# Two encoder layers on one Trainium2 core: norm factors applied behind the first product, projections scaled at eviction, residual rows in large loads, and new spans for the attention

## The chip, the core and the metric

The kernel runs on one core of a Trainium2 chip. The core has TensorE (PE, matrix products into PSUM), VectorE (DVE), ScalarE (ACT), GpSimd (POOL), and SyncE (SP), whose queue issues nearly all DMA transfers here. Each engine works through its own list of instructions in the order in which it stands. The metric is the time of one execution in microseconds (us); lower is better.

## What is computed

Two layers of a streaming encoder over 1024 prompt tokens and 32 sample tokens, model width 1024. Before and behind every sublayer stands an RMS norm; the residual is added behind the second one.

```python
def rms_norm(x, g):
    xf = x.astype(jnp.float32)
    y = xf * lax.rsqrt(jnp.mean(xf * xf, axis=-1, keepdims=True) + EPS)
    return (y * g.astype(jnp.float32)).astype(x.dtype)

def layer_prompt(x, mem, p, t5_table, lam_init):
...
    z = split_in(rms_norm(x, g[N_MIX_PRE]), p['w_in'])
...
    x = x + rms_norm(jnp.concatenate([a, b, c], axis=-1) @ p['w_out'], g[N_MIX_POST])
    mk, mv = mem_kv(mem, g[N_MEM], p['w_mk'], p['w_mv'])
    x, conv_state = tail_sublayers(x, mk, mv, jnp.zeros((B, CONV_W - 1, D_FF), x.dtype), p)

def tail_sublayers(x, mk, mv, conv_past, p):
    g = p['norms']
    x = x + rms_norm(cross_attention(rms_norm(x, g[N_X_PRE]), mk, mv, p['w_xq'], p['w_xo']), g[N_X_POST])
    f, conv_state = conv_ffn(rms_norm(x, g[N_F_PRE]), conv_past, p['w_gate'], p['w_up'],
                             p['conv_w'], p['conv_b'], p['w_down'])
    return x + rms_norm(f, g[N_F_POST]), conv_state
```

`a`, `b` and `c` are three groups of attention heads (differential, banded, latent), which read parts of `z`. The sample tokens attend to caches of 1024 older tokens.

## The kernel before

**Tiles.** Activations lie with the model width on the partitions: eight tiles of 128 rows, one column for each token. The tokens are cut into two halves, h = 0 of 544 columns (the chunks g = 0 and 1, of 256 and 288; the 32 sample tokens sit in the second) and h = 1 of 512 (two chunks of 256). A product runs in fp32r: every operand is split into a high part (`hi`, a copy, line 118 on ACT) and a low part (`lo`, the difference, line 137 on POOL or 135 on DVE), and `mm3` (lines 217 to 219) issues three matmuls for each pair of tiles. `unit` is one 128-row tile of a product over the whole width: 24 matmuls into one PSUM tile `ps_g`.

**Names of stages.** The text calls project(l,h) the input projection of a layer and half (22 tiles of w_in), attention (l,h) what `attend` does, cross (l,h) what `cross` does: the output projection w_out with its norms, the query product w_xq, the cross attention into 256 memory tokens, its product w_xo with its norms; ffn (l,h) is the gated MLP, and its end `finish` is the last down product with its norms.

**Two streams.** `run` makes one program out of two generators. `dense` yields project(0,0), the first norm of half 1, the memory keys, project(0,1), and then ffn(l,h) and project(l+1,h) in turn. `latent` yields for each (l,h) the attention and then the cross. `par` always continues the generator whose time, summed from the yields, is behind: a positive yield is PE work, a negative one is waiting, and a yielded function holds the generator until it is true. `paced` spreads the attention over `SPANS`; `slowed(gen, k)` adds waiting of k times the work; `ffn` starts when `"done" in F[l, h]`. So these numbers alone decide how many matmuls of the dense stream stand in PE's list beside one step of the latent stream. What stands there is called filler here.

**Norms.** `sum_squares` squares eight tiles on ACT (line 244) and adds them on DVE and POOL (line 246); `inv_rms` sums over the partitions by a matmul with `ones` (line 254, on PE) and takes the inverse root on ACT (lines 233 and 234). `prenorm` waits for this factor r, multiplies x, gain and r (line 399, DVE) and splits; all of it stands ahead of the first product. `prenorm_late` (cross and ffn) splits x times gain at once and issues the sum of squares and the matmul of line 254 behind that but ahead of the first product; the product is multiplied by r at its eviction. `postnorm` multiplies by gain and r (line 469) and adds the residual (line 470), which `residual` loads by four DMAs of two tiles (`xr`, two buffers) for each chunk.

**Evictions.** The projections' PSUM tiles are copied by ACT (`z_k`, `z_v`, `z_cq`, `z_ckv`) or split by ACT and DVE (`z_q`). The gate product of the ffn is multiplied by r in line 1652 on DVE.

## Time and profile before

| | us |
|---|---|
| median of three runs | 3716.85 (3716.11 to 3724.8) |
| the profiled execution, its own time | 3728.03 |
| its span in the trace | 3725.5 |
| PE busy | 3266.1 (88%) |
| DVE, ACT, POOL busy | 2073.0, 1836.3, 2080.5 |

The span runs from the first to the last recorded instruction; the profiled execution took 11.18 us more than the median. PE is the busiest engine. A matmul is pipelined with its neighbours, so a busy PE is not always a PE at its peak; the count of matmuls in a stretch tells more than the busy time.

### The profile page before, as it was taken

The page shows a single profiled execution, that of the slowest core. Times are in us where ns is not written, and L with a number is a line of the kernel's source. Part 1 is how long each engine was busy: PE and PEld are TensorE (multiplying, and loading weights), DVE is VectorE, ACT ScalarE, POOL GpSimd, SP SyncE. Part 2 cuts the span into 40 slices and gives each one's busy share as a digit, 9 for nine tenths or more (in the row PEclk, how much of TensorE's full clock was granted, in tenths as well). Part 3 has the DMA queues.
Part 4 walks back from the last instruction along what each step waited for, and adds up shares of the span by engine and source line. Part 5 has one row for each costly group of instructions (what it writes and reads, how often), then busy time and mean ns, then how long its engine had stood idle before and what let it go on. Part 6 is the DMA issues. An engine that isn't in the chain of part 4 may idle for free.

```text
span 3725.5 us, 66150 instructions
## 1 busy us (share of the span) xinstructions
PE 3266.1 (88%) x24536; PEld 3099.4 (83%) x24536; DVE 2073.0 (56%) x4627; ACT 1836.3 (49%) x3926; POOL 2080.5 (56%) x1868
## 2 busy tenths in 40 slices
PE   6997997699999799759999969959999998579997
PEld 5986896599999699659999959959998998579996
DVE  4665316576676743365666562557787654554444
ACT  3565535555454545455445453466555453543332
POOL 5444545476665545546665565656565466556654
PEclk9997997799999799879999989979999999789998
DMA  7665643133333455413334444433344343122222
GB/s 221 215 187 152 205 158 121 63 109 93 110 110 104 143 183 173 132 56 108 118 121 127 134 132 164 165 112 105 105 125 119 109 122 120 53 80 86 86 86 80
DMA packets 246505, 464.79 MB, mean 125 GB/s; under 512 B 42513, under 2 KB 136105, under 8 KB 246185
## 3 DMA queue, kind: packets, MB, share of 16 engines
q1 hardware_dynamic: 243736, 457.07, 39.1%
q8 instruction: 194, 3.18, 0.3%
q0 software_dynamic: 2448, 3.51, 0.3%
q14 instruction: 127, 1.03, 0.1%
HBM read 365.93 MB, written 97.66 MB: 124 GB/s over the span
## 4 chain that ended last, share of the span: by engine, by line
PE 64%; DVE 14%; ACT 7%; DMA 6%; issue 4%; POOL 4%; SPq 1%; POOLq 0%; ACTq 0%; DVEq 0%
PE ps_g L217 17%; PE ps_g L218 17%; PE ps_g L219 16%; DVE gt L1676 4%; PE ps_g L575 3%; DVE pg L469 2%; PE ps_g L651 2%; PE ps_g L650 1%; PE ps_g L254 1%; PE ps_sc L716 1%; DMA xr<-x 1%; ACT wh L118 1%; DVE pg L412 1%; POOL wl L137 1%; DVE zn L246 1%
## 5 line engine op out<-in xcount | busy, mean ns | idle before, releaser
L217 PE MATMUL ps_g<-pg,wh 128*128 128x256 f32 (+1 forms) x4352 | 1260.2, 290 | 20.2 <-ACT pg L118 17.1
L218 PE MATMUL ps_g<-pg,wh 128*128 128x256 f32 (+1 forms) x4352 | 1251.9, 288 | 5.3 <-POOL pg L137 3.9
L219 PE MATMUL ps_g<-pg,wl 128*128 128x256 f32 (+1 forms) x4352 | 1246.2, 286 | 0.0
L137 POOL TENSOR_TENSOR wl<-wr,wh 128x1024 fp32r<-128x1024 f32 (+1 forms) x368 | 885.6, 2411 | 457.7 <-ACT wh L118 437.2
L217 PEld LDWEIGHTS ps_g<-pg,wh 128*128 128x128 f32 x4352 | 828.4, 190 | 30.2 <-ACT pg L118 20.2
L218 PEld LDWEIGHTS ps_g<-pg,wh 128*128 128x128 f32 x4352 | 826.6, 190 | 10.0 <-POOL pg L137 5.3
L219 PEld LDWEIGHTS ps_g<-pg,wl 128*128 128x128 f32 x4352 | 822.9, 189 | 0.2
L118 ACT ACTIVATE wh<-wr 128x1024 fp32r<-128x1024 f32 (+1 forms) x368 | 383.4, 1053 | 555.7 <-PE ps_g L218 402.9
L217 PE MATMUL ps_g<-hs,wh 128*128 128x256 f32 (+1 forms) x1424 | 417.4, 299 | 45.3 <-DVE pg L1712 39.7
L218 PE MATMUL ps_g<-hs,wh 128*128 128x256 f32 (+1 forms) x1424 | 410.7, 290 | 4.5 <-POOL hs L137 4.4
L219 PE MATMUL ps_g<-hs,wl 128*128 128x256 f32 (+1 forms) x1424 | 408.2, 289 | 0.0
L673 ACT ACTIVATE pg<-ps_sc,sm 128x640 f32<-128x640 f32 (+7 forms) x384 | 278.0, 729 | 125.0 <-DVE sm L724 73.8
L217 PEld LDWEIGHTS ps_g<-hs,wh 128*128 128x128 f32 x1424 | 271.2, 193 | 64.6 <-DVE pg L1712 48.7
L1676 DVE SCALAR_TENSOR_TENSOR gt<-gt,cst,gt 128x32 f32<-128x32 f32 (+3 forms) x264 | 272.3, 1050 | 74.5 <-ACT gt L1671 73.2
L1712 DVE TENSOR_TENSOR pg<-pg,ps_g 128x256 f32<-128x256 f32 (+1 forms) x640 | 260.3, 422 | 89.4 <-PE ps_g L219 87.2
L118 ACT ACTIVATE pg<-ps_g 128x512 fp32r<-128x512 f32 (+3 forms) x480 | 209.2, 455 | 186.4 <-PE ps_g L575 171.9
L135 DVE TENSOR_TENSOR pg<-ps_g,pg 128x512 fp32r<-128x512 f32 (+2 forms) x448 | 225.7, 518 | 101.7 <-ACT pg L118 99.3
L218 PEld LDWEIGHTS ps_g<-hs,wh 128*128 128x128 f32 x1424 | 275.7, 194 | 7.1 <-POOL hs L137 6.1
L219 PEld LDWEIGHTS ps_g<-hs,wl 128*128 128x128 f32 x1424 | 275.5, 193 | 0.2
L217 PE MATMUL ps_g<-pg,pg 128*128 128x256 f32 (+1 forms) x768 | 229.0, 299 | 5.2 <-ACT pg L118 5.2
L575 PE MATMUL ps_g<-ident,pg 128*128 128x128 f32 x1232 | 200.9, 291 | 34.0 <-POOL pg L1550 26.6
L219 PE MATMUL ps_g<-pg,pg 128*128 128x256 f32 (+1 forms) x768 | 225.2, 295 | 1.1 <-POOL pg L137 1.0
(243 smaller groups left out, 6281.5 us busy)
## 6 DMA issues: line engine op xcount, KB each, us to landing
wr<-i_w_in SPq DMA_DIRECT2D x88, 512.0 KB
wr<-i_w_gate SPq DMA_DIRECT2D x88, 512.0 KB
wr<-i_w_up SPq DMA_DIRECT2D x88, 512.0 KB
wr<-i_w_down SPq DMA_DIRECT2D x88, 512.0 KB
pg<-i_w_out SPq DMA_DIRECT2D x32, 512.0 KB
qt<-aq SPq DMA_DIRECT2D x192, 64.0 KB
pg<-av SPq DMA_DIRECT2D x24, 512.0 KB
pg<-ak SPq DMA_DIRECT2D x96, 128.0 KB
```

The lines of the kernel that those rows point to most:

```text
L118: nc.scalar.activation(out, in_, AF.Copy)
L135: nc.vector.tensor_sub(out, in_, h)
L137: nc.gpsimd.tensor_sub(out, in_, h)
L217: nc.tensor.matmul(out, wh, xh, start=(i == 0), stop=False)
L218: nc.tensor.matmul(out, wh, xl, start=False, stop=False)
L219: nc.tensor.matmul(out, wl, xh, start=False, stop=(i == n - 1))
L469: nc.vector.scalar_tensor_tensor(ys[k], ys[k], self.gain(l, which, k), r, op0=ALU.mult, op1=ALU.mult)
L575: self.nc.tensor.transpose(q[:, i * 128 : i * 128 + 128], e[:, c : c + 128], self.ident)
L651: nc.tensor.matmul(p[:, a:b], v(kt), aT[1][s // 4][:, s % 4, a:b], start=False, stop=(i == n - 1))
L673: self.nc.scalar.activation(e[:, :n], sc, AF.Exp, bias=m, scale=-1.0, accum_out=z)
L1676: nc.vector.scalar_tensor_tensor(cv[:, a:b], gp[:, a + o - e : b + o - e], conv_col(f, tap), cv[:, a:b], op0=ALU.mult, op1=ALU.add)
L1712: nc.vector.tensor_add(y[m][:, cols(g)], y[m][:, cols(g)], p)
```

## The change

The second norm form, `prenorm`, goes; `prenorm_late` is used everywhere, and no longer issues the matmul of line 254 itself: it leaves it in `late[chunk]`, and `now` issues it right behind the first unit of the product that follows. The projections' evictions therefore multiply by the factor r (`Xr`), on DVE; the high parts of queries and keys move to ACT and the low part of queries to POOL. `residual` is replaced by `chunk_load`: two or three DMAs for a chunk, issued ahead of the norm, into `pg` pages or, at the end of the ffn, into `gt`, `u` and `hs` tiles. `outputs` loads the attention's results in the same way. The four spans shrink, a page is added (`NPG`) and an `xr` buffer taken, the w_xq loads are issued later, the ffn may start as soon as both its inputs are named, and the cross is slowed by 0.5 in its inner part in place of 1.0 in all. The number of matmuls stays the same.

```diff
-SPANS = (220.0, 480.0, 400.0, 380.0)
+SPANS = (180.0, 400.0, 340.0, 350.0)
...
-NPG = 26
+NPG = 27
...
-    def prenorm(self, xs, l, which, w, out, pages, lo=("pool",)):
-
-        nc = self.nc
-        acc = self.sum_squares(xs, w)
-        yield -5
-        r = self.inv_rms(acc, self.ones, 1024.0, w)
-        yield -2
-        xh, xl = pages()
-        for k in range(KT):
-            a = self.t("st")[:, :w]
-            nc.vector.scalar_tensor_tensor(a, xs[k], self.gain(l, which, k), r, op0=ALU.mult, op1=ALU.mult)
-            self.hi("act", xh[k], a)
-            self.lo(lo[k % len(lo)], xl[k], a, xh[k])
-        out.extend((xh, xl))
-        yield -4
-
-    def prenorm_late(self, xs, l, which, w, r, out, pages):
+    def prenorm_late(self, xs, l, which, w, r, out, pages, late, chunk, wait=0):
+
 
         nc = self.nc
         xh, xl = pages()
@@ -414,8 +399,17 @@
                 yield -2
         acc = self.sum_squares(xs, w)
         out.extend((xh, xl))
-        yield -4
-        self.inv_rms(acc, self.ones, 1024.0, w, r=r)
+        late[chunk] = lambda: self.inv_rms(acc, self.ones, 1024.0, w, r=r)
+        yield -2
+        if wait:
+            yield -wait
+            self.now(late, chunk)
+
+    @staticmethod
+    def now(late, g):
+        f = late.pop(g, None)
+        if f:
+            f()
...
+    def chunk_load(self, src, g, tiles=None):
+
+        w, out = width(g), []
+        if tiles is None:
+            n = 2 * HW[0] // w
+            tiles = [(self.t("pg"), min(n, KT - k)) for k in range(0, KT, n)]
+        for page, n in tiles:
+            x = page[:, : n * w].rearrange("p (k c) -> p k c", k=n)
+            k = len(out)
+            self.dma(x, src[k : k + n, :, span(g)].rearrange("k p c -> p k c"))
+            out += [x[:, i] for i in range(n)]
         return out
 
-    def postnorm(self, ys, l, which, src, g, out, store=None):
+    def postnorm(self, ys, l, which, xs, g, out, store=None):
...
-        xs = self.residual(src, g) if not isinstance(src, list) else src
+        yield -7
...
             g = 2 * h + c
             p = self.ps("g")[:m, : width(g)]
             self.unit(w, self.Xc[c], p, m)
+            self.now(self.late, g)
             evac(p, g)
...
+        nc, r = self.nc, self.Xr
         def evac(p, g):
-            self.hi("act", z[:, 0, cols(g)], p, scale)
-            self.lo("dve", z[:, 1, cols(g)], p, z[:, 0, cols(g)], scale)
+            cs = cols(g)
+            a = self.t("st")[:, : width(g)]
+            nc.vector.scalar_tensor_tensor(a, p, scale, r[:, cs], op0=ALU.mult, op1=ALU.mult)
+            self.hi("act", z[:, 0, cs], a)
+            self.lo("pool", z[:, 1, cs], a, z[:, 0, cs])
...
-            nc.scalar.activation(raw[:, cs], p, AF.Copy)
-            self.hi("dve", z[:, 0, cs], raw[:, cs])
+            nc.vector.tensor_mul(raw[:, cs], p, r[:, cs])
+            self.hi("act", z[:, 0, cs], raw[:, cs])
...
-                nc.scalar.activation(raw[:, cols(g)], p, AF.Copy)
+            def evac(p, g, raw=raw):
+                nc.vector.tensor_mul(raw[:, cols(g)], p, r[:, cols(g)])
...
+            nc.gpsimd.tensor_mul(a, a, rx[:32, cs])
...
         def split(p, a):
             self.hi("act", oh[p], a)
             self.lo("pool", ol[p], a, oh[p])
 
-        xs = load(0) + load(2)
-        yield -2
+        xs = list(enumerate(self.chunk_load(d.od, g)))
+        yield -3
...
-        for p, a in load(4) + load(6):
+        for p, a in xs[4:]:
...
-            if m + 1 < KT:
-                ws = split(raw)
+                yield -1.5
+                if m + 1 < KT and g == G[0]:
+                    nxt = split(raw)
+            ws = nxt
         O.clear()
         del pages
-        raws = [load("w_xq", m) for m in range(2)]
...
+            xs = self.chunk_load(d.xin, g)
+            yield from self.postnorm(ys, l, 1, xs, g, ys)
+            del xs
             if g == G[0]:
-                yield -3
-                wq.extend(split(raw) for raw in raws)
-            yield from self.postnorm(ys, l, 1, d.xin, g, ys)
+                raws = [load("w_xq", m) for m in range(2)]
             if g == G[1]:
                 yield lambda: ("q", G[0]) in done
             xn = []
-            yield from self.prenorm_late(ys, l, 2, w, rr[:, cs], xn, lambda: self.chunk_pages(w))
-            yield -2
+            late = {}
+            yield from self.prenorm_late(ys, l, 2, w, rr[:, cs], xn, lambda: self.chunk_pages(w), late, g)
             if not q:
+                wq.extend(split(raw) for raw in raws)
                 q.extend(self.pair_pages())
+                yield -3
             for m in range(2):
                 p = self.ps("g")[:, :w]
                 self.unit(wq[m], xn, p)
+                self.now(late, g)
                 a = self.t("st")[:, :w]
                 nc.vector.scalar_tensor_tensor(a, p, scale, rr[:, cs], op0=ALU.mult, op1=ALU.mult)
                 self.hi("act", q[0][m][:, cs], a)
@@ -1595,7 +1597,7 @@
...
             F[g] = []
-            yield from self.prenorm_late(ys, l, 4, w, F["r"][:, cols(g)], F[g], lambda: fp(g))
+            yield from self.prenorm_late(ys, l, 4, w, F["r"][:, cols(g)], F[g], lambda: fp(g), F["late"], g, 10)
 
         fp = self.half_pages()
         wx = []
-        yield from self.par(*[self.seq(queries(g), attention(g % 2), rest(g)) for g in G])
-        F["done"] = True
+        yield from self.slowed(self.par(*[self.seq(queries(g), attention(g % 2), rest(g)) for g in G]), 0.5)
...
             self.unit(wts["g", f], F[g], p)
+            self.now(F["late"], g)
...
+        last = l + 1 == DEPTH
+        if not last:
+            self.Xc, self.late, self.Xr = [[], []], {}, self.t("r")
         pages = self.half_pages()
 
         def finish(g):
             ys = [t[:, cols(g)] for t in y]
+            if g == gs[0]:
+                xs = self.chunk_load(d.x2, g, [(self.t("gt"), 2) for _ in range(3)] + [(self.t("u"), 2)])
             yield from down_units(k, ws, g)
-            yield from self.postnorm(ys, l, 5, d.x2, g, ys, d.x3)
-            if l + 1 < DEPTH:
-                yield from self.prenorm(ys, l + 1, 0, width(g), self.Xc[g % 2], lambda: pages(g), ("pool", "dve"))
+            if g == gs[1]:
+                xs = self.chunk_load(d.x2, g, [(self.t("hs"), n) for n in (3, 3, 2)])
+            yield from self.postnorm(ys, l, 5, xs, g, ys, d.x3)
+            if not last:
+                yield from self.prenorm_late(ys, l + 1, 0, width(g), self.Xr[:, cols(g)], self.Xc[g % 2], lambda: pages(g),
+                                             self.late, g)
 
...
-                yield lambda: "done" in F[l, h]
+                yield lambda: all(F[l, h].get(g) for g in (2 * h, 2 * h + 1))
...
-                yield from self.slowed(self.cross(l, h, F[l, h]), 1.0)
+                yield from self.cross(l, h, F[l, h])
```

In the rows below an operation is shown as its line in that version, then output<-inputs by the program's names, then the shape.

**PE, cross (0,1), between the last w_out product (ps_g_17822) and the first query product.** In the version before, in its last rows `ps_g_18009` is that query product:

```order
L217 MATMUL ps_g_17822<-pg_16547,pg_17792 128x256
L218 MATMUL ps_g_17822<-pg_16551,pg_17792 128x256
L219 MATMUL ps_g_17822<-pg_16547,pg_17793 128x256
L254 MATMUL ps_g_17911<-zn_17853,ones 128x256
L254 MATMUL ps_g_17940<-zn_17882,ones 128x256 x2
L254 MATMUL ps_g_18002<-zn_17981,ones 128x256
L217 MATMUL ps_g_18009<-pg_17961,pg_17874 128x256
L218 MATMUL ps_g_18009<-pg_17963,pg_17874 128x256
L219 MATMUL ps_g_18009<-pg_17961,pg_17875 128x256
```

In the changed version, the same engine where the sums of squares (zn, ones) of the first postnorm and of the chunk behind it stand; `ps_g_17341` and `ps_g_17377` are units of project(1,0):

```order
L217 MATMUL ps_g_17341<-pg_15190,wh_17270 128x256
L218 MATMUL ps_g_17341<-pg_15194,wh_17270 128x256
L219 MATMUL ps_g_17341<-pg_15190,wl_17271 128x256
L254 MATMUL ps_g_17367<-zn_17221,ones 128x256 x2
L254 MATMUL ps_g_17372<-zn_17246,ones 128x256
L217 MATMUL ps_g_17377<-pg_15187,wh_17270 128x288
L218 MATMUL ps_g_17377<-pg_15191,wh_17270 128x288
L219 MATMUL ps_g_17377<-pg_15187,wl_17271 128x288
```

Before, three sums of squares stand one behind the other between the w_out product and the query product. Now units of the projection stand on both sides of them; in all, the matmuls of other stages between the last w_out and the first w_xo product of a cross go from 221 to 494 in cross (0,0), from 0 to 400 in (0,1), from 666 to 1062 in (1,0) and from 0 to 52 in (1,1).

**PE, the start of ffn (0,0), behind cross (0,0).** Before (L716 are scores of the attention (0,1), `ps_g_7997` is the first gate unit):

```order
L254 MATMUL ps_g_7800<-zn_7712,ones 128x256 x2
L254 MATMUL ps_g_7866<-zn_7805,ones 128x288 x2
L716 MATMUL ps_sc_8128<-pg_7978,qt_7982 128x512
L716 MATMUL ps_sc_8128<-pg_7978,qt_7982 128x384
L716 MATMUL ps_sc_8212<-pg_7974,qt_7982 128x512
L716 MATMUL ps_sc_8212<-pg_7974,qt_7982 128x384
L254 MATMUL ps_g_7932<-zn_7879,ones 128x256 x2
L254 MATMUL ps_g_7966<-zn_7945,ones 128x288
L217 MATMUL ps_g_7997<-pg_7850,wh_6984 128x256
L218 MATMUL ps_g_7997<-pg_7854,wh_6984 128x256
L219 MATMUL ps_g_7997<-pg_7850,wl_6985 128x256
```

And in the changed version, where `ps_g_7948` is the first gate unit and `ps_g_7979` the second:

```order
L217 MATMUL ps_g_7948<-pg_7831,wh_7211 128x256
L218 MATMUL ps_g_7948<-pg_7835,wh_7211 128x256
L219 MATMUL ps_g_7948<-pg_7831,wl_7212 128x256
L717 MATMUL ps_sc_8318<-pg_8170,qt_8174 128x512
L717 MATMUL ps_sc_8318<-pg_8170,qt_8174 128x384
L717 MATMUL ps_sc_8392<-pg_8166,qt_8174 128x512
L717 MATMUL ps_sc_8392<-pg_8166,qt_8174 128x384
L254 MATMUL ps_g_7973<-zn_7857,ones 128x256 x2
L217 MATMUL ps_g_7979<-pg_7828,wh_7211 128x288
L218 MATMUL ps_g_7979<-pg_7832,wh_7211 128x288
L219 MATMUL ps_g_7979<-pg_7828,wl_7212 128x288
```

The scores and the sum of squares of chunk 0 (`ps_g_7973`) have moved behind the first gate unit, of which the last three matmuls are shown; the second unit stands directly behind them.

**SP, the end of the program.** Before, from the last weight of the down product on (`x_1_124` is the residual in HBM, `o_y` the result):

```order
L108 DMA wr_42210<-i_w_down 128x1024
L108 DMA wr_42271<-i_w_down 128x1024
L108 DMA o_y<-pg_38408 128x256
L108 DMA o_y<-pg_38409 128x256
L108 DMA xr_42485<-x_1_124 128x2x256
L108 DMA xr_42487<-x_1_124 128x2x256
L108 DMA o_y<-pg_38408 128x256
L108 DMA o_y<-pg_38409 128x256
L108 DMA o_y<-pg_38410 128x256
L108 DMA o_y<-pg_38411 128x256
L108 DMA o_y<-pg_38410 128x256
L108 DMA o_y<-pg_38411 128x256
```

And in the changed version:

```order
L108 DMA wr_42128<-i_w_down 128x1024
L108 DMA gt_42250<-x_1_124 128x2x256
L108 DMA u_42253<-x_1_124 128x2x256
L108 DMA wr_42189<-i_w_down 128x1024
L108 DMA gt_42251<-x_1_124 128x2x256
L108 DMA hs_42407<-x_1_124 128x3x256
L108 DMA gt_42252<-x_1_124 128x2x256
L108 DMA hs_42408<-x_1_124 128x3x256
L108 DMA hs_42409<-x_1_124 128x2x256
L108 DMA o_y<-pg_38326 128x256
L108 DMA o_y<-pg_38327 128x256
L108 DMA o_y<-pg_38328 128x256
```

The seven residual loads stand ahead of the first store; before, the loads of two tiles stand between stores.

At the end of an ffn that a projection follows, the matmuls of other stages between the last down product and the first projection product go from 96 to 115 for (0,0) and from 55 to 152 for (0,1).

## Rows read from the trace of the kernel before

**Rows 1.** The page: busy time of each engine; the granted clock in 40 slices.

```profile
PE 3266.1 (88%) x24536; PEld 3099.4 (83%) x24536; DVE 2073.0 (56%) x4627; ACT 1836.3 (49%) x3926; POOL 2080.5 (56%) x1868
...
PEclk9997997799999799879999989979999999789998
```

**Rows 2.** Stretches of the core: busy time, granted clock, DMA share, GB/s.

```profile
core 0: us, PE busy (x) PEld busy (x) DVE busy (x) ACT busy (x) POOL busy (x), PEclk, DMA share, GB/s
...
455.00:567.00 112.00, 112.00 (x923) 111.95 (x922) 15.65 (x18) 40.05 (x75) 55.90 (x32) 1.00 0.47 160
567.00:729.00 162.00, 100.20 (x589) 87.10 (x587) 103.55 (x183) 88.28 (x234) 85.77 (x100) 0.71 0.30 98
729.00:1228.00 499.00, 485.77 (x3717) 470.13 (x3716) 336.69 (x780) 253.78 (x449) 305.60 (x243) 1.00 0.35 105
1228.00:1302.00 74.00, 50.67 (x266) 40.08 (x265) 58.22 (x138) 39.28 (x99) 39.20 (x41) 0.75 0.48 142
...
1530.00:1679.00 149.00, 85.89 (x533) 75.78 (x533) 83.45 (x167) 78.25 (x206) 78.10 (x86) 0.73 0.26 83
...
2156.00:2225.00 69.00, 36.76 (x227) 31.03 (x226) 46.08 (x95) 39.74 (x108) 38.50 (x42) 0.78 0.44 133
...
2347.00:2520.00 173.00, 128.67 (x918) 118.84 (x917) 101.14 (x187) 98.19 (x248) 96.44 (x103) 0.85 0.40 134
...
3147.00:3289.00 142.00, 72.40 (x435) 63.27 (x433) 89.18 (x170) 71.18 (x192) 72.90 (x84) 0.69 0.25 76
...
3687.00:3725.50 38.50, 14.17 (x106) 12.68 (x104) 19.39 (x47) 8.80 (x21) 14.21 (x16) 0.75 0.31 96
```

**Rows 3.** The same view: pieces of 2347 to 2520, cross (1,0).

```profile
2347.00:2404.00 57.00, 51.72 (x411) 50.74 (x411) 39.74 (x60) 31.28 (x70) 36.60 (x30) 0.97 0.52 180
2404.00:2447.00 43.00, 40.74 (x315) 37.81 (x314) 19.21 (x35) 21.91 (x59) 23.61 (x30) 0.96 0.44 138
2447.00:2476.00 29.00, 14.79 (x80) 11.33 (x78) 9.69 (x26) 18.71 (x53) 18.59 (x23) 0.73 0.35 122
2476.00:2493.50 17.50, 17.16 (x108) 15.74 (x107) 6.68 (x18) 10.86 (x29) 5.08 (x8) 0.85 0.00 0
2493.50:2520.00 26.50, 4.26 (x12) 3.22 (x11) 25.82 (x51) 15.43 (x37) 12.56 (x14) 0.52 0.41 134
```

**Rows 4.** Waits of PE, whole span: total us, times, longest.

```profile
PE ps_g L254 <- DVE zn L246: 91.7, 16, 21.3
PE ps_sc L716 <- DMA pg<-ak: 64.8, 3, 22.5
```

**Rows 5.** Waits of PE in 1228 to 1302.

```profile
PE ps_g L254 <- DVE zn L246: 17.2, 2, 8.7
```

**Rows 6.** Waits of PE in 2156 to 2225.

```profile
PE ps_g L254 <- ACT zn L244: 24.8, 2, 19.2
```

**Rows 7.** The chain that ended last: start, us, DMA pieces of it.

```profile
10.51 6.95 DMA wr<-i_w_in
...
1273.40 5.55 DMA xr<-x
1281.57 4.27 DMA xr<-x
...
3705.95 2.66 DMA xr<-x
3712.74 2.87 DMA xr<-x
3717.77 3.57 DMA xr<-x
```

**Rows 8.** DVE groups by form: count, busy us, mean ns, idle before.

```profile
L469 DVE SCALAR_TENSOR_TENSOR pg<-pg,cst,zn 128x256 f32<-128x256 f32 x144 | 83.7, 649 | 6.9 <-ACT zn L234 6.9
L1652 DVE TENSOR_TENSOR gt<-ps_g,r 128x256 f32<-128x256 f32 x176 | 74.5, 423 | 259.9 <-PE ps_g L219 254.2 <-ACT r L234 5.5
```

**Rows 9.** Line 469: durations, smallest, median, largest.

```profile
L469 DVE SCALAR_TENSOR_TENSOR pg<-pg,cst,zn x192: 469/485/2633, 586.7 to 3708.9; 128x256 f32<-128x256 f32 x144, 128x288 f32<-128x288 f32 x48
```

More of the change, by code (lines that the diff above doesn't have):

```diff
@@ L83 @@
     BUFS = dict(pg=NPG, wr=2, wh=3, wl=3, zn=4, ob=2, st=3, qt=2, sm=8,
-                strip=2, sst=1, qb=1, sg=1, kn=2, vn=1, sel=3, hs=3, gt=3, u=1, xr=2, r=2)
+                strip=2, sst=1, qb=1, sg=1, kn=2, vn=1, sel=3, hs=3, gt=3, u=1, xr=1, r=2)
     COLS = dict(pg=2 * HW[0], wr=1024, wh=1024, wl=1024, zn=2 * CB,
@@ L448, in half_pages @@
         return get
-    def residual(self, src, g):
-        out = []
-        w = width(g)
-        for k in range(0, KT, 2):
-            x = self.t("xr").rearrange("p (k c) -> p k c", k=2)
-            self.dma(x[:, :, :w], src[k : k + 2, :, span(g)].rearrange("k p c -> p k c"))
-            out += [x[:, i, :w] for i in range(2)]
+    def chunk_load(self, src, g, tiles=None):
[8 more added lines that the diff above has]
+            out += [x[:, i] for i in range(n)]
         return out
-    def postnorm(self, ys, l, which, src, g, out, store=None):
+    def postnorm(self, ys, l, which, xs, g, out, store=None):
         nc, w = self.nc, width(g)
         acc = self.sum_squares(ys, w)
-        yield -5
-        xs = self.residual(src, g) if not isinstance(src, list) else src
+        yield -7
         r = self.inv_rms(acc, self.ones, 1024.0, w)
@@ L536, in z_v @@
         nc = self.nc
-        raw = self.t("gt")
+        raw, r = self.t("gt"), self.Xr
         def evac(p, g):
-            nc.scalar.activation(raw[:, cols(g)], p, AF.Copy)
+            nc.vector.tensor_mul(raw[:, cols(g)], p, r[:, cols(g)])
         yield from self.z_tile(l, mt, h, evac)
@@ L1119, in z_cq @@
         for m in range(2):
-            raw = self.t("gt")
+            raw, r = self.t("gt"), self.Xr
             cq.append(raw)
-            def evac(p, g):
-                nc.scalar.activation(raw[:, cols(g)], p, AF.Copy)
+            def evac(p, g, raw=raw):
+                nc.vector.tensor_mul(raw[:, cols(g)], p, r[:, cols(g)])
             yield from self.z_tile(l, 18 + m, h, evac)
@@ L1128, in z_ckv @@
         nc, io = self.nc, self.io
-        page = self.t("gt")
+        page, rx = self.t("gt"), self.Xr
         out.append(page)
@@ L1134, in evac_kv @@
             raw = page[:, cols(g)]
-            nc.scalar.activation(raw, p, AF.Copy)
+            nc.vector.tensor_mul(raw, p, rx[:, cols(g)])
             norms.append((g, raw, self.sum_squares([raw], width(g))))
@@ L1424, in outputs @@
         oh, ol = pages(g)
-        def load(p):
-            x = self.t("xr").rearrange("p (k c) -> p k c", k=2)
-            self.dma(x[:, :, :w], d.od[p : p + 2, :, span(g)].rearrange("k p c -> p k c"))
-            return [(p + i, x[:, i, :w]) for i in range(2)]
         def split(p, a):
@@ L1597, in rest @@
                 wx.extend(split(raw) for raw in wraw)
-                F["r"] = self.t("r")
+                F["r"], F["late"] = self.t("r"), {}
                 yield -4
@@ L1767, in first_norm @@
     def first_norm(self, h, y):
-        self.Xc = [[], []]
+        self.Xc, self.late, self.Xr = [[], []], {}, self.t("r")
         pages = self.half_pages()
         def chunk(g):
-            yield from self.prenorm([t[:, cols(g)] for t in y], 0, 0, width(g), self.Xc[g % 2], lambda: pages(g), ("pool", "dve"))
+            yield from self.prenorm_late([t[:, cols(g)] for t in y], 0, 0, width(g), self.Xr[:, cols(g)], self.Xc[g % 2],
+                                         lambda: pages(g), self.late, g)
         yield from self.par(*[chunk(g) for g in (2 * h, 2 * h + 1)])
```

3 lines of the change are left out of this document (1 added, 2 removed).

## The prediction, made before the changed kernel ran

> **What bounds the kernel now.** I read the page's busy times first, then the granted clock by slices: PE is busy 3266.1 of 3725.5 us, no other engine over 56%, and the clock row falls from 9 to 7 only in some slices [rows 1]. So the kernel is a PE kernel with holes, and the question is where these lie. The windows answer it. In 455 to 567 PE issues 923 matmuls in 112.00 us without a gap at clock 1.00, which is 0.1213 us for one [rows 2]. I call the loss of a stretch its length less its matmuls times 0.1213. Seven stretches hold most of it: cross (0,0) 567 to 729, 162 − 589 × 0.1213 = 90.5; the end of ffn (0,0) 1228 to 1302, 41.7; cross (0,1) 1530 to 1679, 84.3; the end of ffn (0,1) 2156 to 2225, 41.5; cross (1,0) 2347 to 2520, 61.6; cross (1,1) 3147 to 3289, 89.2; the end 3687 to 3725.5, 25.6. Together 434. In each the granted clock is low too (0.69 to 0.85), while in ffn (0,0), 729 to 1228, PE is busy 485.77 of 499 at 1.00 [rows 2].
>
> The reader should then look at cross (1,0), since it is the one cross that already has filler (666 matmuls of other stages), and at where its loss still sits [rows 3]: 2347 to 2447, which has filler, loses 7.1 + 4.8; 2447 to 2476, where 80 matmuls of its own stand alone, 19.3 (clock 0.73); 2476 to 2493.5, the w_xo product, 4.4; 2493.5 to 2520, the last norms, 25.0. It is the measure of what filler leaves. The waits name the causes: the sum-of-squares matmul waits for DVE's sums in line 246 for 91.7 us, and scores of the next attention wait three times, up to 22.5 us, for their load (L716, 64.8) [rows 4].
>
> **The change part by part.** The matmuls remain the same, so PE's own work does not shrink; the loss does, as far as holes are filled.
>
> *The four crosses.* Spans and slowing now place filler where there was none, as the order rows of cross (0,1) show. I price each cross by the pieces of cross (1,0): 12 for the filled part, 4 for w_xo, and for the last norms 25.0 less the 24 matmuls of the first gate unit that now stand ahead of their sums (2.9), thus 22. What differs is the part of the cross attention that stays without filler, priced by its count. Cross (0,0): 198 uncovered matmuls in a row become 68, about the 80 that cost 19.3; 12 + 19 + 4 + 22 = 57, saves 33. Cross (0,1): (84.3 − 25 − 4)/312 = 0.177 lost for each of 312 uncovered, now 56, thus 10; 12 + 10 + 4 + 22 = 48, saves 36. Cross (1,0): 68 become none; I leave 3 for it; 41, saves 21. Cross (1,1) has little filler, because ffn (1,0) stands ahead of it and no projection follows: (89.2 − 25 − 4)/313 = 0.192 each, now 212, thus 41; with 4 and 22, and 7 for its postnorm, whose DVE work now meets that of the end of ffn (1,0): 74, saves 15. Sum 105.
>
> *The ends of ffn (0,0) and (0,1).* In the first, PE waits 17.2 us in two pieces for line 246 [rows 5], and the chain that ended last runs there through residual loads, 5.55 and 4.27 [rows 7]. These loads are now issued before the last down product, and the first projection unit stands ahead of the norm's matmul; there are 19 more filler matmuls (2.3). I take 20 of the 41.7 (bounds 9.8, the loads alone, and 30). In the second, the sums of the attention's results wait 24.8 us for ACT's squares [rows 6], whose loads stand on SP behind residual loads; they are now issued in two or three DMAs, and 97 more filler matmuls (11.8) stand there: 27 (bounds 12 and 35).
>
> *The very end.* The chain holds three residual loads, 2.66 + 2.87 + 3.57 = 9.1 [rows 7], which stood between stores on SP; now all seven go ahead of the stores: 8.
>
> *Loads of the attention's results elsewhere:* three crosses, some 1 to 2 us each, 4.
>
> *The start.* The chain goes through the first weight load (6.95 us at 10.51) [rows 7], which does not change: nothing.
>
> Gains: 105 + 20 + 27 + 8 + 4 = 164.
>
> *What it costs.* 168 evictions pass from ACT to DVE and 8 are new. The nearest row is line 1652, the same kind of operation (PSUM times r): 176 of 256 columns at 423 ns [rows 8], in the ffn, where PE is kept busy. 176 × 0.423 = 74 us of DVE, spread over four projections, with DVE busy 56% over the span [rows 1]: nothing, and if the cover were gone, each product of 24 matmuls (2.9 us) still leaves room for it. The first evictions wait for r; two PSUM tiles are held for a few us, eight times. Fewer DMAs stand on SP, 1811 for 1843; but loads into `gt`, `u` and `hs` wait for the last readers of these tiles, and weight loads queue behind them. A weight is used later than the down product that runs then, so nothing. A single `xr` buffer leaves eight pairs of rotary rows waiting 3 to 5 us, an estimate from the residual loads' 3.57 to 5.55 [rows 7], off the path.
>
> The filler comes from somewhere: 273 + 400 + 396 + 52 = 1121 matmuls, 136 us of PE, leave stretches in which they covered attention. If these are left bare, up to all of it is given back; if enough remains, nothing. I take 10, since a filled stretch loses 7.1 of 57 us at most [rows 3], and the attention's spans shrink as well, which draws matmuls of its own forward.
>
> Net 154. The profiled execution took 3728.03 with a span of 3725.5; so 3574 for it. It stands 11.2 above the median of before, thus a median of 3563; I say **3560**, its own range 3500 to 3615.
>
> **The rivals.**
>
> *The filler is missed elsewhere (R1).* Half of the 136 us comes back, as holes in projection or attention stretches: 3560 + 58 = 3620, range 3600 to 3690. For it: PE's list is fixed, and attention squeezed from 480 to 400 waits on softmax chains of DVE and ACT. Against: 729 to 1228 holds attention at 3717 matmuls and is still full.
>
> *DVE and POOL slow each other down (R2).* The 256-column form of line 469 has a mean of 649 ns [rows 8] where the median of all 192 is 485 and the longest 2633 [rows 9]: it is slowed in norms, where POOL adds and splits. With filler the norms are no longer what PE waits for, but two norm chains now run at once (cross (1,1) with the end of ffn (1,0)) and more low parts go to POOL. Thirty-two DVE operations of a norm at 0.164 us more are 5 us, over eight norms 42: 3600. The Trainium skill, page "SBUF — State Buffer", section "Who interferes with whom", says that a DVE instruction with two SBUF inputs contends with a GpSimd instruction that reads SBUF; the trace agrees, with 649 against 485 ns. By that rule alone the time is this rival's 3600, with the rows' cover it is 3560; and the added evictions, whose product comes from PSUM, would be free of it.
>
> *More is saved (R3).* The last norms of the crosses also fill, since the scores that waited for their load (L716, 64.8 us in three waits) [rows 4] now have a gate unit ahead and a page more: three times 22 goes, with some of the rest: 3480.
>
> *Slower (R4).* DVE's evictions bind the projections: DVE works in order, and a PSUM tile waits behind norm or softmax work of up to 2.6 us (the longest of line 469) [rows 9]. It decides from the point at which PE loses 154/176 = 0.9 us per eviction; at 1.3 it is 3790. Against: line 1652, as many, in a full ffn.
>
> *No effect (R5).* PE is in order, and the filler may stand behind the same sum it was to cover: PE still waits the 91.7 us of line 246, later. Within 11 us of 3717, the 0.3% which this kernel's times can tell from no change.
>
> **How the numbers follow.** Forecast 0.54, R1 0.18, R2 0.08, R3 0.10, R4 0.06, R5 0.04. The time is that of the first. The range 3480 to 3680 leaves out R4 and R5 (0.10), the top of R1 (0.04) and half of R3 (0.04). Faster: all but R4 and R5, 0.90; same 0.04; slower 0.06.
>
> **What would show it.** In windows over the four crosses, PE's loss falls to about 57, 48, 41 and 74, at a clock over 0.9 in the first three. L254's waits for line 246 fall below 50 us; no wait and no piece of the chain names a load into `xr` from x. R1 would show as new waits of PE in projections (line 217 for splits, scores for ACT); R2 as a mean of line 469 above 0.65 us; R3 if L716's waits for `ak` vanish; R4 if line 217 waits for DVE's evictions of `gt`. I am wrong if attention falls short of its filler, or if the loads into `gt` and `hs` come late and hold the weights behind them.

## The result, and the profile after

The changed kernel takes 3627.98 us (median of three, 3626.44 to 3628.3) where the kernel before takes 3716.85: a ratio of 0.9754, with an interval of 0.9731 to 0.9776. The profiled execution took 3626.44 us with a span of 3624.7, 100.8 less than the span before. The median lies inside the range, 68 us above the forecast of 3560.

The page of the changed kernel, the rows that answer to [rows 1]:

```profile
PE 3262.4 (90%) x24536; PEld 3105.2 (86%) x24536; DVE 2070.7 (57%) x4667; ACT 1810.9 (50%) x3854; POOL 2088.8 (58%) x1892
...
PEclk8997998799999989979999999989999999689998
```

Windows of the changed kernel: the four crosses up to the third gate unit of the ffn (528, 1462, 2212 in four pieces, 3061.5), ffn (0,0) and (0,1) behind them, the ends of both, the stretch of the w_out product of cross (0,1) at 1305.5, and the end. Columns as in [rows 2]:

```profile
528.00:720.00 192.00, 143.15 (x936) 132.05 (x935) 113.12 (x198) 97.88 (x243) 106.08 (x112) 0.81 0.32 106
720.00:1243.00 523.00, 511.16 (x3871) 489.50 (x3870) 369.14 (x863) 275.96 (x504) 306.38 (x257) 1.00 0.38 114
1243.00:1305.50 62.50, 47.80 (x280) 42.24 (x278) 53.94 (x112) 40.61 (x94) 38.22 (x32) 0.84 0.46 140
1305.50:1462.00 156.50, 155.64 (x1244) 153.85 (x1244) 34.36 (x67) 64.36 (x132) 88.44 (x70) 1.00 0.55 181
1462.00:1624.00 162.00, 126.66 (x816) 115.41 (x815) 105.19 (x197) 94.70 (x242) 98.93 (x103) 0.82 0.32 106
1624.00:2118.00 494.00, 478.79 (x3877) 456.09 (x3876) 299.72 (x770) 255.70 (x560) 300.53 (x291) 0.99 0.41 127
2118.00:2180.50 62.50, 49.00 (x351) 47.20 (x350) 42.99 (x70) 32.64 (x74) 40.16 (x32) 0.91 0.42 135
2212.00:2297.00 85.00, 72.29 (x520) 69.78 (x520) 49.75 (x68) 34.28 (x70) 52.16 (x42) 0.88 0.36 128
2297.00:2403.00 106.00, 101.33 (x803) 96.77 (x802) 39.35 (x84) 52.65 (x132) 66.68 (x70) 0.95 0.52 171
2403.00:2415.50 12.50, 12.05 (x95) 11.84 (x95) 6.00 (x14) 9.31 (x26) 8.30 (x10) 1.00 0.52 186
2415.50:2450.50 35.00, 18.48 (x87) 15.24 (x86) 30.48 (x60) 21.03 (x48) 16.68 (x18) 0.71 0.32 102
3061.50:3204.50 143.00, 80.99 (x457) 69.25 (x456) 99.84 (x184) 76.05 (x203) 78.62 (x88) 0.69 0.15 51
3593.00:3624.70 31.70, 14.38 (x107) 12.79 (x105) 21.77 (x47) 8.77 (x21) 13.39 (x16) 0.81 0.36 116
```

The loss as the prediction defines it, from these rows: crosses 192 − 936 × 0.1213 = 78.5, 63.0, 55.9 and 87.6, against 90.5, 84.3, 61.6 and 89.2 before; the ends of the ffns 28.5 and 19.9, against 41.7 and 41.5; the very end 18.7, against 25.6. The crosses' windows reach to the ffn's third unit here because its first unit waits for the same norm; that makes little difference, since windows of before up to the third unit (739 us in ffn (0,0)) give 90.5, 83.1, 63.2 and 89.9.

One difference counts. All four windows here begin at the last w_out product of the cross, but those of before begin 30 us ahead of it in cross (0,1) and 23 us ahead in (1,1). From the last w_out product to the third gate unit the kernel before loses 172.0 − 664 × 0.1213 = 91.5 us, 127.5 − 413 × 0.1213 = 77.4, 197.5 − 1110 × 0.1213 = 62.9 and 128.5 − 407 × 0.1213 = 79.1. Like for like the crosses therefore save 13, 14 and 7 us and cross (1,1) loses 8.5 more, 26 saved in sum. The rest stands in the stretches ahead: from ffn (0,0)'s end to the last w_out product of (0,1) the loss goes from 258.0 − 1887 × 0.1213 = 29.1 to 5.6, and from the end of cross (1,0) to that of (1,1) from 639.5 − 4615 × 0.1213 = 79.7 to 611.0 − 4566 × 0.1213 = 57.1.

In crosses (0,0) and (0,1), the piece with filler up to the last query product, and the attention behind it:

```profile
528.00:614.00 86.00, 71.92 (x521) 69.96 (x520) 54.42 (x71) 34.64 (x74) 52.30 (x44) 0.90 0.33 110
614.00:671.00 57.00, 37.69 (x231) 31.99 (x231) 24.45 (x56) 34.24 (x98) 33.17 (x44) 0.76 0.39 127
...
1462.00:1540.00 78.00, 68.06 (x477) 64.91 (x476) 52.07 (x81) 40.99 (x99) 51.97 (x47) 0.89 0.29 97
1540.00:1579.00 39.00, 28.08 (x162) 23.69 (x162) 19.65 (x42) 25.91 (x73) 25.37 (x32) 0.78 0.46 150
```

PE's waits over the whole span (total us, times, longest):

```profile
PE ps_g L218 <- DVE pg L397: 46.4, 18, 7.8
...
PE ps_g L217 <- ACT pg L396: 21.1, 5, 4.9
...
PE ps_g L553 <- DVE gt L540: 11.1, 2, 6.7
PE ps_g L254 <- DVE zn L246: 10.8, 8, 3.7
...
PE ps_sc L717 <- DMA pg<-ak: 3.0, 3, 1.5
```

The reader is to see that the waits of [rows 4] are nearly gone, 91.7 to 10.8 and 64.8 to 3.0, and that the loss at the end of a cross is not: the piece from the last w_xo product on, 25.0 in [rows 3], is 24.4 at 2415.5. PE now waits there within the first gate unit, for the high parts (L396, ACT) and low parts (L397, DVE) of x times gain. One chain, another name.

### The profile page after: what moved, and what is told of

It is laid out like the page before. It is cut to its first block, busy times and chain, and to the rows that moved or that the text cites. A ratio compares the mean times of both kernels' runs of the same rounds, so it can differ in the third digit from the quotient of the medians.

```text
span 3624.7 us, 66135 instructions
## 1 busy us (share of the span) xinstructions
PE 3262.4 (90%) x24536; PEld 3105.2 (86%) x24536; DVE 2070.7 (57%) x4667; ACT 1810.9 (50%) x3854; POOL 2088.8 (58%) x1892
## 4 chain that ended last, share of the span: by engine, by line
PE 63%; DVE 15%; ACT 6%; issue 4%; DMA 3%; POOL 3%; SPq 0%; DVEq 0%; ACTq 0%; POOLq 0%
PE ps_g L217 17%; PE ps_g L218 16%; PE ps_g L219 16%; DVE gt L1678 3%; PE ps_g L576 3%; DVE pg L465 3%; DVE pg L397 2%; PE ps_g L652 2%; PE ps_g L651 2%; DVE pg L466 1%; PE ps_g L254 1%; ACT wh L118 1%; PE ps_sc L717 1%; DVE pg L1714 1%; DVE sm L724 1%
## 5 line engine op out<-in xcount | busy, mean ns | idle before, releaser
L217 PE MATMUL ps_g<-pg,wh 128*128 128x256 f32 (+1 forms) x4352 | 1274.6, 293 | 54.2 <-ACT pg L396 19.3
L218 PE MATMUL ps_g<-pg,wh 128*128 128x256 f32 (+1 forms) x4352 | 1263.0, 290 | 37.3 <-DVE pg L397 36.4
L217 PEld LDWEIGHTS ps_g<-pg,wh 128*128 128x128 f32 x4352 | 837.8, 193 | 67.6 <-ACT pg L396 21.0
L218 PEld LDWEIGHTS ps_g<-pg,wh 128*128 128x128 f32 x4352 | 836.1, 192 | 45.2 <-DVE pg L397 39.8
L219 PEld LDWEIGHTS ps_g<-pg,wl 128*128 128x128 f32 x4352 | 832.6, 191 | 0.3
L1714 DVE TENSOR_TENSOR pg<-pg,ps_g 128x256 f32<-128x256 f32 (+1 forms) x640 | 261.6, 421 | 107.6 <-PE ps_g L219 105.6
L1678 DVE SCALAR_TENSOR_TENSOR gt<-gt,cst,gt 128x32 f32<-128x32 f32 (+3 forms) x264 | 248.7, 964 | 65.1 <-ACT gt L1673 64.3
L217 PE MATMUL ps_g<-pg,pg 128*128 128x256 f32 (+1 forms) x768 | 225.1, 293 | 27.8 <-ACT pg L118 25.4
L576 PE MATMUL ps_g<-ident,pg 128*128 128x128 f32 x1232 | 200.2, 289 | 42.3 <-POOL pg L1552 19.5
```

The source lines that it names most:

```text
L217: nc.tensor.matmul(out, wh, xh, start=(i == 0), stop=False)
L218: nc.tensor.matmul(out, wh, xl, start=False, stop=False)
L219: nc.tensor.matmul(out, wl, xh, start=False, stop=(i == n - 1))
L576: self.nc.tensor.transpose(q[:, i * 128 : i * 128 + 128], e[:, c : c + 128], self.ident)
L1678: nc.vector.scalar_tensor_tensor(cv[:, a:b], gp[:, a + o - e : b + o - e], conv_col(f, tap), cv[:, a:b], op0=ALU.mult, op1=ALU.add)
L1714: nc.vector.tensor_add(y[m][:, cols(g)], y[m][:, cols(g)], p)
```

## The experiments

All times are medians. In brackets stands the 95% interval of the ratio to runs of the kernel before on the same chip (3718.5, 3719.0 and 3719.4 us in the three groups). Differences to the changed kernel's 3627.98 are between groups, whose kernels before differ by up to 3 us. There are twelve runs; the first three take the change apart.

**loads_alone**: before, with `chunk_load` alone.

```diff
-        xs = self.residual(src, g) if not isinstance(src, list) else src
+        # at the head of queries(g), ahead of postnorm
+            xs = self.chunk_load(d.xin, g)
...
-NPG = 26
+NPG = 27
```

> The kernel before with the large early loads alone (residuals and attention results; 27 pages and one xr buffer, as these loads need); norms, evictions and the numbers of the order as before. Theory A (the order's numbers make most of the gain, the loads a part): the ends of the two ffns and the very end lose the waits for residual loads, 10 + 8 + 9 us, so 3690 us. Rival B (the late norm is what frees the ends of the ffns, the loads were hidden anyway): within 0.3% of 3717.

Measured: 3688.93 (0.9907 to 0.9934). The loads alone give 30 us; rival B falls. They come only in part at the places that theory A names: the very end gains 7 (31.6 us in place of 38.5 for its last matmuls) and the end of ffn (0,0) 6, the end of ffn (0,1) nothing (the table at norm_first); the pieces of crosses (0,1) and (1,1) up to the last query product gain 6 and 7.

**loads_order**: the same with the new spans and slowing.

```diff
-SPANS = (220.0, 480.0, 400.0, 380.0)
+SPANS = (180.0, 400.0, 340.0, 350.0)
...
-                yield from self.slowed(self.cross(l, h, F[l, h]), 1.0)
+                yield from self.cross(l, h, F[l, h])
```

> The large loads, and the spans and slowing of the change, but norms ahead of the product and evictions on ACT as before, and the ffn starting at done. Theory A: the shortfall against the forecast is that filler's evictions on DVE stand behind norm work, so without them the filled pieces of the crosses lose 12 and not 25: 3600 to 3625 us, not slower than the changed kernel's 3628. Rival B (late norms and evictions carry the gain): 3670 or more.

Measured: 3660.11 (0.9828 to 0.9855). Between both: order on top of the loads gives 29 us, and what I expected, no loss against the changed kernel, was wrong by 32. The run does not price the evictions on DVE, since the waiting yielded in the norms differs too and filler falls on other places: the piece of cross (1,0) up to the last query product holds 416 matmuls here (84.2 us) and 520 in the changed kernel (85.0).

**order_old**: the changed kernel with the old numbers (the reverse of the last diff, and `"done"`).

> The changed kernel with the spans, the slowing and the start of the ffn of the kernel before. Theory A: only loads and late norms remain: 3670 to 3690 us, and crosses (0,0), (0,1) lose what they lost before (some 95 and 88 us). Rival B: 3640 or less, since the order's numbers are a small part.

Measured: 3681.4 (0.9887 to 0.9914). So the rest of the change (late norms, evictions on DVE, the later split of w_xq) gives only 7 us over the loads on the old order (3688.9 to 3681.4), but 32 on the new one (3660.1 to 3628.0). Not all of it was without gain on the old order: the ends of the ffns lose less (the table at norm_first), but cross (1,0) lost filler, and its piece up to the last query product loses 72.4 − 338 × 0.1213 = 31.4 us where loads_alone loses 87.0 − 669 × 0.1213 = 5.9. Scores also still wait for their load as in [rows 4], since no gate unit stands ahead of them.

```profile
PE ps_sc L717 <- DMA pg<-ak: 64.8, 3, 22.4
```

**evict_pool**: the changed kernel, projections copied by ACT and multiplied on POOL.

```diff
-            nc.vector.tensor_mul(raw[:, cs], p, r[:, cs])
+            nc.scalar.activation(raw[:, cs], p, AF.Copy)
+            nc.gpsimd.tensor_mul(raw[:, cs], raw[:, cs], r[:, cs])
```

> The changed kernel with the projections' evictions copied by ACT and multiplied by r on POOL in place of DVE. Theory A: PE's waits for L519 and L540 on DVE go, the query pieces of crosses (0,0) and (1,0) lose 10 us less each: 3605 us. Rival C (these waits only come from where the filler stands; another engine's queue is as long): 3628, and up to 3650 with 134 us more work on POOL, whose weight splits of 2.4 us stand ahead.

Measured: 3640.07 (0.9777 to 0.9804), 12 slower than the change. PE's transposes of values now wait for POOL's multiplication (waits of PE, this run):

```profile
PE ps_g L556 <- POOL gt L543: 13.5, 2, 8.1
...
PE ps_g L550 <- POOL gt L543: 12.0, 5, 5.8
```

The queue moved, and POOL's is no shorter: rival C.

**Where an eviction stands on DVE.** The query piece of cross (1,0), 2212 to 2297, loses 85 − 520 × 0.1213 = 21.9 where I forecast 12 for it and what follows. PE's waits there, in the changed kernel:

```profile
PE ps_g L553 <- DVE gt L540: 6.7, 1, 6.7
PE ps_g L217 <- DVE gt L519: 4.0, 1, 4.0
```

DVE's timeline of the changed kernel at that place (start, us, operation):

```profile
2244.51 2.67 DVE L397 SCALAR_TENSOR_TENSOR pg<-pg,cst,pg 128x256 fp32r<-128x256 f32 x1
2247.10 2.59 DVE L466 TENSOR_TENSOR pg<-pg,pg 128x288 f32<-128x288 f32 x1
2249.61 0.41 DVE L519 TENSOR_TENSOR gt<-ps_g,r 128x256 f32<-128x256 f32 x1
2249.95 3.16 DVE L466 TENSOR_TENSOR pg<-pg,pg 128x288 f32<-128x288 f32 x2
2253.03 0.41 DVE L540 TENSOR_TENSOR gt<-ps_g,r 128x256 f32<-128x256 f32 x1
```

And POOL's:

```profile
2244.51 2.39 POOL L137 TENSOR_TENSOR pg<-pg,pg 128x1024 fp32r<-128x1024 f32 x1 [0.97 <-ACT pg L118]
2246.86 2.52 POOL L137 TENSOR_TENSOR wl<-wr,wh 128x1024 fp32r<-128x1024 f32 x1
2249.34 2.56 POOL L137 TENSOR_TENSOR pg<-pg,pg 128x1024 fp32r<-128x1024 f32 x1
```

The reader is to see that L519 and L540, the evictions for which PE waits, take 0.41 us, and that norm operations in front of them (L397, L466) take 2.67 and 2.59, run beside a POOL operation and end 0.3 behind its end; L397 alone takes 0.47. Two of these three POOL operations are the low parts of w_xq (`pg<-pg`, 128x1024), which the change has moved from ahead of the postnorm to here. That gave the next test.

**wxq_early**: the changed kernel with w_xq loaded and split as before.

```diff
+        raws = [load("w_xq", m) for m in range(2)]
...
             xs = self.chunk_load(d.xin, g)
+            if g == G[0]:
+                yield -3
+                wq.extend(split(raw) for raw in raws)
...
             if not q:
-                wq.extend(split(raw) for raw in raws)
```

> The changed kernel with the w_xq weights loaded behind w_out and split ahead of the first postnorm of the cross, as before. Theory F (the wait of 18.9 us of the first query product in cross (1,1) is for this split, queued on ACT behind squares): that wait shrinks by 10 us or more, 3615 us. Rival G (the split only stands last in a chain that the norm sets; the product then waits for the low parts on DVE): 3628 within 11 us.

Measured: 3584.28 (0.9626 to 0.9653), 44 us faster than the change, more than I expected, and elsewhere: cross (1,1) gains 5. Windows of this run, the crosses and the query piece of (1,0):

```profile
530.50:706.00 175.50, 136.18 (x930) 125.12 (x929) 109.83 (x199) 98.63 (x246) 107.00 (x113) 0.84 0.34 114
1450.00:1604.00 154.00, 121.56 (x814) 110.48 (x814) 104.98 (x197) 93.20 (x241) 99.48 (x103) 0.86 0.35 112
2192.00:2270.50 78.50, 73.42 (x583) 72.15 (x582) 48.75 (x74) 36.85 (x78) 59.12 (x50) 0.98 0.49 160
2192.00:2416.50 224.50, 198.94 (x1501) 189.60 (x1500) 122.63 (x231) 118.28 (x279) 146.94 (x140) 0.92 0.48 155
3025.50:3163.50 138.00, 80.81 (x456) 69.62 (x456) 96.72 (x186) 75.72 (x207) 74.54 (x88) 0.70 0.16 53
```

The query piece loses 78.5 − 583 × 0.1213 = 7.8 in place of 21.9, and the four crosses 62.7, 55.3, 42.4 and 82.7, together 42 less than in the changed kernel. That piece of cross (0,0) loses 8.9 (574 matmuls in 78.5 us) in place of 22.8, but the one of (0,1) still 17.6 (473 in 75.0) in place of 20.1. PE's waits in the piece of (1,0):

```profile
PE ps_g L553 <- DVE gt L540: 4.1, 1, 4.1
PE ps_g L217 <- DVE gt L519: 0.7, 1, 0.7
```

These two waits shrink by 5.9 of the 14 us; the granted clock of the piece goes from 0.88 to 0.98. The edit brings back a `yield -3` with the split, so filler moves too: 583 matmuls stand in the piece where 520 stood, though the whole cross holds as many as in the changed kernel (1501 and 1499).

**wxq_load**: only the load goes back, the split stays late.

> The changed kernel with the w_xq weights loaded behind w_out, as before, but split where the change splits them, behind x times gain. Theory H (what costs 44 us is the place of the split: two POOL operations of 2.5 us each stand among the norm's, hold DVE, and the projection's evictions queue behind): 3628 within 11 us. Rival I (the load lands late, 5 to 8 us behind its issue, and the split waits for it): most of the 44 us comes back, 3590.

Measured: 3628.42 (0.9743 to 0.9769). The load's place costs nothing. What costs the 44 us is where the split stands, together with the 3 us of waiting that wxq_early sets beside it; no run parts these two.

**pool512** and **pool256**: each weight tile's low part in two or four operations.

```diff
-        self.lo("pool", l[:, :n], raw[:, :n], h[:, :n])
+        for c in range(0, n, 512):
+            s = slice(c, min(n, c + 512))
+            self.lo("pool", l[:, s], raw[:, s], h[:, s])
```

> The changed kernel with POOL's low part of each weight tile (128x1024, 2.4 us) cut into two operations of 512 columns. Theory D (the filled pieces of the crosses lose 25 us because DVE's norm operations, and the evictions queued behind them, are held up to 2.6 us by one such POOL operation): a hold is halved, the 256-column mean of line 465 falls from 755 ns to 600 or less, the query pieces lose 5 us less each, 3610 us. Rival E (POOL holds DVE as long in sum, whatever the length of one operation): 3628 within 11 us, mean of line 465 as it was.

> The same in four operations of 256 columns. POOL has some 370 x 0.7 us = 260 us more to do. Theory D: line 465 at 550 ns, and the time near 3610 unless POOL becomes what weights wait for. Rival E: slower than 3628 by what the weight splits now lack, 3640 to 3700.

Measured: 3595.45 (0.9657 to 0.9685) and 3593.47 (0.9653 to 0.9679), 33 and 35 us faster than the change; yet the mean of line 465 (line 467 in these two runs) goes from 755 ns only to 753 and 744, as rival E had it. Mean and then smallest, median and largest in the changed kernel, pool512 and (the last line) pool256:

```profile
L465 DVE SCALAR_TENSOR_TENSOR pg<-pg,cst,zn 128x256 f32<-128x256 f32 x144 | 99.5, 755 | 11.5 <-ACT zn L234 11.5
L467 DVE SCALAR_TENSOR_TENSOR pg<-pg,cst,zn 128x256 f32<-128x256 f32 x144 | 99.2, 753 | 13.1 <-ACT zn L236 13.1
```

```profile
L465 DVE SCALAR_TENSOR_TENSOR pg<-pg,cst,zn x192: 470/506/2659, 541.8 to 3617.0; 128x256 f32<-128x256 f32 x144, 128x288 f32<-128x288 f32 x48
L467 DVE SCALAR_TENSOR_TENSOR pg<-pg,cst,zn x192: 468/508/1548, 544.6 to 3585.0; 128x256 f32<-128x256 f32 x144, 128x288 f32<-128x288 f32 x48
L467 DVE SCALAR_TENSOR_TENSOR pg<-pg,cst,zn x192: 469/939/1337, 546.5 to 3580.8; 128x256 f32<-128x256 f32 x144, 128x288 f32<-128x288 f32 x48
```

The longest hold shrinks with POOL's operation, the holds in sum do not. The pieces of crosses (0,0), (0,1) and (1,0) up to the last query product lose 3, 1 and 4 us less with the halves (19.5, 19.2 and 18.3), short of the 5 each of theory D. Most of the gain lies elsewhere: in ffn (1,1), where PE waits nine times, 17.6 us, for the down product's additions (L1714). The changed kernel's DVE there:

```profile
3268.39 2.12 DVE L1678 SCALAR_TENSOR_TENSOR gt<-gt,cst,gt 128x512 f32<-128x512 f32 x1 [1.76 <-ACT gt L1673]
3270.43 1.07 DVE L1714 TENSOR_TENSOR pg<-pg,ps_g 128x256 f32<-128x256 f32 x3
3271.42 0.74 DVE L1678 SCALAR_TENSOR_TENSOR gt<-gt,cst,gt 128x512 f32<-128x512 f32 x1
```

The convolution's operation on 512 columns (L1678) takes 2.12 us in one place and 0.74 in the next; a POOL operation of 2.37 us ran from 3267.59. The additions stand behind it. Windows of ffn (1,1), the changed kernel and the kernel `combo` below, which has the halves:

```profile
3204.50:3593.00 388.50, 370.54 (x3010) 368.47 (x3009) 162.26 (x295) 135.66 (x187) 239.17 (x171) 0.96 0.26 85
```

```profile
3158.00:3525.00 367.00, 359.27 (x3009) 357.02 (x3008) 149.54 (x295) 136.64 (x187) 257.68 (x233) 1.00 0.29 91
```

PE's waits in these two windows:

```profile
PE ps_g L217 <- DVE pg L1714: 17.6, 9, 2.0
```

```profile
PE ps_g L219 <- DVE pg L1719: 7.6, 9, 0.9
```

As many matmuls in 367.0 in place of 388.5 us. Of these 21.5 us the shorter waits are 10; the other 11 are PE's own busy time, 370.54 and 359.27, at a clock of 0.96 and 1.00.

**before_pool512**: the halves in the kernel before.

> The kernel before with POOL's low part of each weight tile in two halves. If the 33 us which this gave the changed kernel have nothing to do with the change (most of it lay in ffn (1,1), where the down product's additions on DVE are held): the same here, 3685 to 3690 us. If they are a part of what the change costs (queries and norms behind POOL): 3710 or more.

Measured: 3687.04 (0.9896 to 0.9926), 32 us, of which ffn (1,1) has 22 (388.5 to 366.3 us): this gain was open before the change and has no part in it.

**norm_first**: the projections' sum-of-squares matmul ahead of their first unit.

```diff
+            self.now(self.late, g)
             self.unit(w, self.Xc[c], p, m)
-            self.now(self.late, g)
```

> The changed kernel with the projections' sum-of-squares matmul ahead of their first unit in place of behind it; the ffn and the queries keep it behind. If standing behind the first product is what the ends of the ffns gain by: (0,0) and (0,1) lose 3 to 10 us more each and the start some, 3640 us or more. If the early split of x times gain does it and the place of the matmul does not matter: 3628 within 11 us.

Measured: 3630.85 (0.9745 to 0.9782), no change that the interval tells. The traces still show something at the ends of the ffns. The same 250 matmuls, from the end of the last down product on, take (us):

| | before | loads_alone | order_old | changed | norm_first |
|---|---|---|---|---|---|
| ffn (0,0) | 69.2 | 62.7 | 58.0 | 56.7 | 61.1 |
| ffn (0,1) | 71.1 | 71.3 | 64.8 | 45.7 | 47.0 |

At the end of (0,0) the loads give 6, what order_old adds to them (late norms above all) 5 and the new order 1; putting the matmul ahead takes 4 back, within the forecast 3 to 10. At the end of (0,1) the loads give nothing, order_old 6 and the new order 19; the matmul ahead takes 1 back. What the early split of x times gain does by itself was not run.

**combo** (w_xq early and halves) and **combo_spans** (still shorter spans):

> The changed kernel with the w_xq split early and POOL's weight splits in halves. If both lie in different places: 3628 - 44 - 26 to 33 = 3550 to 3560 us. If both shorten the same holds in the crosses, 3570 or more.

> The same with still shorter spans (150, 340, 290, 320). If filler in the crosses is still short: 5 to 20 us less than the kernel without it. If the attention then lacks filler of its own (the give-back that the prediction feared): slower than it by 10 us or more.

Measured: 3555.95 (0.9546 to 0.9574) and 3560.26 (0.9555 to 0.9588). The two gains nearly add up (44 and 33, together 72); combo is 163 us below the kernel before. Shorter spans change nothing that these intervals tell apart.

## Why the prediction was right or wrong

**The reading of before** held where it looked: the losses were where the windows showed them, and they shrank at each place that was named but cross (1,1). The list was not complete, though: the seven stretches hold 434 of the 749 us that the span loses by the same price. 240 to 423 (965 matmuls, 66 us) and 2520 to 3049 (3870, 60 us) stood in no term, and the change left nearly all of it.

**The ends and the loads** came within their bounds. The ends of the ffns saved 13 and 22 for 20 and 27, the very end 7 for 8. The mechanism held for the very end and in part for (0,0), where the loads by themselves gave 6. For (0,1) it was half right: the attention's loads gave nothing there alone, and most came with the new order (the table at norm_first), whose filler I had put at 11.8. The whole of the loads gave 30 when run alone. The w_out stretches ahead of crosses (0,1) and (1,1) saved 23 each, where I had 4 for three such places. So places that I had priced at next to nothing made up for part of the crosses' shortfall, and the time inside the range is in part luck.

**The crosses** are the step that failed. I forecast 33 + 36 + 21 + 15 = 105; the rows give 12.0 + 21.3 + 5.7 + 1.6 = 41, and like for like only 26. My sign of a clock over 0.9 in the first three did not come either: 0.81, 0.82 and 0.89. The step is first "12 for the filled part": the filled query pieces lose 20 to 23. Its cause is largely an edit that my working named in no term, the later split of w_xq. With it undone, and its 3 us of waiting with it, the crosses save 27.8 + 29.0 + 19.2 + 6.5 = 82 by the same windows (68 like for like), and the pieces lose 8.9, 17.6 and 7.8: the price of 12 then serves for (0,0) and (1,0), not for (0,1). The run with the load alone shows that the load has no part in it. That the path runs from POOL's split over DVE's held norm operations to the evictions queued behind them is read from the timelines of one cross; the shorter waits of PE when the split moves fit it. What parts the added ACT operations of the split and the moved filler had is open, and halving all of POOL's weight splits took only 1 to 4 us from these pieces. The second mis-sized term is the attention behind the queries, priced by the few matmuls left uncovered: 19 and 10 in (0,0) and (0,1), measured 57 − 231 × 0.1213 = 29.0 and 39 − 162 × 0.1213 = 19.3. Its cause is open. I had called the rotary loads into the single `xr` buffer off the path, but the chain that ended last holds three of them, 5.36 us at 638.67, 3.31 at 1557.38 and 2.73 at 2401.46; two buffers were not tried.

**The last norms**, 22 forecast, lose 22.4 to 24.6. The unit put ahead of the sum of squares works only as far as its operands exist, and these come out of the same chain.

**R1** had the time that came, but not the cause. Its give-back shows as 53.4 − 47.2 = 6 us in ffn (0,0) and 23.7 − 12.5 = 11 in (0,1) (both from the third gate unit on), 17 for the 10 that I took. The windows of before for it:

```profile
739.00:1228.00 489.00, 475.77 (x3642) 460.24 (x3642) 333.14 (x773) 249.47 (x441) 302.49 (x239) 1.00 0.36 107
1687.50:2156.00 468.50, 459.96 (x3759) 440.00 (x3759) 280.78 (x740) 236.04 (x497) 287.77 (x272) 1.00 0.40 125
```

In combo_spans, shorter spans do not change the time.

**R2**'s mechanism was at work, at a place that I had not thought of. Its sign came: the mean of line 465, which was line 469, is 755 ns, 649 before [rows 8]. I had priced it by the norms' own length, and dismissed it because norms with filler are not waited for; filler's evictions behind them are. The mean says little of the price, though: with the early split, 44 us faster, it is still 739 ns.

**R3**: its sign came too, the waits for `ak` fell to 3.0 us, but without the time, since PE waits for the high and low parts next. So this sign was badly chosen: the loss of the stretch would have told.

**R4** as a price was far off: an eviction takes 0.40 to 0.46 us (line 540 below). As a queue it is part of what happened: PE waits 11.1 us for L540, in two pieces.

The Trainium skill, page "SBUF — State Buffer", section "Who interferes with whom", has the rule that a DVE instruction with two SBUF inputs contends with a GpSimd instruction that reads SBUF. The trace agrees: the evictions, whose product comes from PSUM, keep one duration in 48 executions, and the low parts of x times gain, with two inputs in SBUF, go up to 2670 ns. Of line 397 on 256 columns, the 79 with no POOL operation on two tensors beside them take 484 ns at most; the 65 with one have a median of 942. Smallest, median and largest in the changed kernel:

```profile
L540 DVE TENSOR_TENSOR gt<-ps_g,r x48: 401/425/458, 38.1 to 2350.4; 128x256 f32<-128x256 f32 x36, 128x288 f32<-128x288 f32 x12
```

```profile
L397 DVE SCALAR_TENSOR_TENSOR pg<-pg,cst,pg x192: 465/476/2670, 6.5 to 3195.2; 128x256 fp32r<-128x256 f32 x144, 128x288 fp32r<-128x288 f32 x48
```

What stays open: cross (1,1) was to gain 15 and like for like loses 8.5 us more than before, 3.6 more with the early split. Its postnorm meets the one at the end of ffn (1,0) on DVE, which I had priced at 7. The price may be far too small: the piece up to the last query product loses 65.5 − 171 × 0.1213 = 44.8 us in the changed kernel, 54.0 − 132 × 0.1213 = 38.0 in the kernel before and 42.4 − 134 × 0.1213 = 26.1 in order_old, where most of that end stands ahead of it. But order_old pays for the end there, and the meeting was not tried alone.

## What to carry to other kernels

Price every instruction that a change moves, also where its count stays the same, by what shares its engine and its operands' memory at the new place: the later split, with two POOL operations of 2.5 us in each cross, cost most of 44 us here. Matmuls put into a hole bring their evictions along, and these can queue behind the very work that made the hole. When a wait disappears from the list, look at the loss of its stretch before believing that the time is won.
